# Experts' rows by indirect DMA: gathered from DRAM, and seven of sixteen pairs' outputs scattered to a DRAM table and added at the end

## The chip, the cores and the metric

The kernel runs on one core of one Trainium2 chip. The metric is the device time of one execution in microseconds, as the median of three runs. The profile is of one further execution; its times are counted from the first instruction.

## The reference, cut to what matters

One transformer block over 512 tokens of width 1024. A hybrid mixer (a short convolution, a sparse attention, a gated delta rule) adds to x; then a mixture of experts adds to it. The change is about the experts:

```python
h = rms_norm(x, norm_ffn)                       # x: 512 x 1024, after the mixer
grp = argmax(h @ w_rg + b_rg)                   # one of 4 groups of 8 experts
top_p, top_i = top_k(softmax(le[grp]), 2)       # two experts of that group
gate = top_p / sum(top_p) * p_grp
for each expert e and each token t that chose it:
    y[t] += gate[t, e] * (silu(h[t] @ w_eg[e]) * (h[t] @ w_eu[e])) @ w_ed[e]
out = x + y                                     # 32 experts, 1024 x 512, 1024 x 512, 512 x 1024 each, float32
```

## The kernel before

Tokens lie on the 128 partitions in four tiles (t = 0 to 3). The mixer's stages take the first 630 us; TensorE is kept busy in them by products of the input with w_in, w_gate and w_branch, with the attention and the delta rule in between. The delta rule (from L371) goes over four chunks c; its scaling factors are small operations on POOL (L333 to L386). The order of each engine's instructions is made when the kernel is built: the framework places an instruction when its inputs, by a simulated timeline, are there, and goes by program order among those that are ready. So what the program writes later can be placed earlier on an engine that is idle.

Routing (L922 to L1019): for each tile t the residual x1 is completed, split into a high and a low float32r part (h2h, h2l), the logits are made, two experts are chosen (oh), and `pos` gets each token's place within its expert (L939). An expert has room for CAP = 64 tokens; a loop at the end (L1252) handles those beyond, and does nothing for these inputs unless an expert has more.

Experts: for a group q of four experts, `choose` (L931) makes a 0/1 selection matrix pm (128 tokens x 256 places) for each t, and `gather_t` (L1044) multiplies h2h and h2l with it, so that TensorE itself collects the rows, already transposed, into PSUM (pxg); `chosen` copies them to SBUF with the gain (xT). `slots_info` (L1180) multiplies the same matrices with the tokens' numbers, scales and gates (pi). The first group's rows are collected before the loop (L1063).

`ffn_up` (L1079) makes gate and up products of one expert side by side into pgu, then silu on ScalarE and the product with the gate on DVE; its `turn` transposes the result. `ffn_down` (L1120) multiplies with w_ed, the two halves of 512 columns side by side in pd; y is split over ScalarE and DVE (`y_parts`, L1113), and `selection` makes a 0/1 matrix of places x tokens. When two experts have their y, `combine` (L1137) lists eight steps (four tiles t, two halves of the columns); each `combine_step` is two products (pc, L1146) and an addition to x1 on DVE (L1148). The steps are woven one by one into the products of the next experts (L1087, L1127).

Weights come in tiles of 1 MB on SyncE's queue (`wchunk`, L1032), six for an expert, into 15 places that the earlier stages have left free; a place is loaded again when TensorE has read it. The last expert's w_ed comes in three pieces, and each piece is combined and stored by itself (L1237 to L1247).

## Time and profile before

| what | value |
|---|---|
| median of 3 runs | 1253.99 us (1253.55 to 1256.53) |
| profiled execution, its own time | 1255.8 us |
| its span, first to last instruction | 1253.7 us |
| granted TensorE clock, mean | 0.994 |
| TensorE busy | 1210.6 us (97%) |
| DVE, ACT, POOL busy | 652.0, 340.6, 62.2 us |
| DMA | 258.17 MB, mean 206 GB/s |

Busy time is time in which the profile shows an instruction of the engine. Matmuls are pipelined, so two of them overlap in the records. A wait is put down to what ended it. PE is TensorE, DVE VectorE, ACT ScalarE, POOL GpSimd, SP SyncE; PEld are weight loads, and a q behind a name is the engine's queue.

### The profile page before, as it was taken

Reading aid. Unit: us, or ns where it says so; the run is one execution under the profiler, and the core shown is the slowest. Engines: PE = TensorE matmul, PEld = TensorE weight load, DVE = VectorE, ACT = ScalarE, POOL = GpSimd, SP = SyncE. Lnnn points to the kernel's source line nnn. Section 1 sums busy time; section 2 is a strip of 40 time slices with the busy share of each in tenths; the row PEclk is TensorE's granted clock in tenths of the full one; section 3 lists DMA queues with packets and bytes.
Section 4 is the critical chain, followed back from the end, with each engine's and each line's share of the span. In section 5 each row is a group of like instructions: output and inputs, shape, how many; then the busy total and the mean of one; then the engine's idle time right before and its main releaser. Section 6 shows DMA issues by size and latency. Waiting matters only on the chain.

```text
span 1253.7 us, 16998 instructions
## 1 busy us (share of the span) xinstructions
PE 1210.6 (97%) x6727; PEld 778.2 (62%) x6728; DVE 652.0 (52%) x1536; ACT 340.6 (27%) x654; POOL 62.2 (5%) x99
## 2 busy tenths in 40 slices
PE   6999999999999999999999999999999998999987
PEld 5887889877888877668996353535353443534333
DVE  5874865865448655643566352534334343333433
ACT  5443433433335446742341101010100101010111
POOL 1001303100100000000040000000000000000000
PEclk9999999999999999999999999999999999999998
DMA  5322332122233221017706999899879889798851
GB/s 211 104 84 85 101 115 93 65 84 68 71 92 97 72 68 35 1 65 286 301 11 234 421 371 395 324 417 379 345 263 354 357 325 382 283 354 324 332 199 69
DMA packets 46435, 258.17 MB, mean 206 GB/s; under 512 B 5008, under 2 KB 8976, under 8 KB 22032
## 3 DMA queue, kind: packets, MB, share of 16 engines
q1 hardware_dynamic: 44928, 254.95, 54.2%
q10 hardware_dynamic: 1424, 2.09, 0.5%
q8 instruction: 54, 0.88, 0.3%
q14 instruction: 29, 0.24, 0.1%
HBM read 254.93 MB, written 2.10 MB: 205 GB/s over the span
## 4 chain that ended last, share of the span: by engine, by line
PE 91%; DVE 4%; ACT 2%; issue 1%; DMA 1%; POOL 0%; SPq 0%; ACTq 0%; POOLq 0%; DVEq 0%
PE pgu L1083 14%; PE pd L1126 8%; PE pmm L183 8%; PE pmm L181 8%; PE pmm L182 8%; PE pgu L1082 7%; PE pc L1146 5%; PE po L818 3%; PE pxg L1045 2%; PE pxg L1046 2%; PE ptp L812 2%; PE pb L182 2%; PE pb L181 2%; PE pb L183 2%; PE pmn L543 1%; PE pmn L541 1%
## 5 line engine op out<-in xcount | busy, mean ns | idle before, releaser
L1082 PE MATMUL pgu<-we,xT 128*64 128x512 f32 x512 | 241.9, 605 | 0.0
L1083 PE MATMUL pgu<-we,xT 128*64 128x512 f32 x512 | 235.8, 602 | 0.0
L183 PE MATMUL pmm<-hTh,lo 128*128 128x512 f32 x432 | 172.1, 398 | 0.2 <-DVE lo L176 0.2
L181 PE MATMUL pmm<-hTh,hi 128*128 128x512 f32 x432 | 171.1, 396 | 0.0
L182 PE MATMUL pmm<-hTl,hi 128*128 128x512 f32 x432 | 170.6, 395 | 0.0
L176 DVE TENSOR_TENSOR lo<-raw,hi 128x1024 fp32r<-128x1024 f32 x82 | 100.5, 1226 | 115.3 <-ACT hi L175 114.1
L175 ACT CAST hi<-raw 128x1024 fp32r<-128x1024 f32 x82 | 86.1, 1050 | 165.3 <-PE pmm L182 96.0
L1148 DVE TENSOR_TENSOR x<-pc,x 128x512 f32<-128x512 f32 (+2 forms) x132 | 83.8, 669 | 82.4 <-PE pc L1146 81.9
L1083 PEld LDWEIGHTS pgu<-we,xT 128*64 128x64 f32 x512 | 64.9, 137 | 97.4 <-issue 95.6
L1126 PE MATMUL pd<-we,aT 128*64 128x512 f32 x496 | 121.3, 599 | 0.0
L1093 ACT ACTIVATE act<-pgu,rss 64x512 f32<-64x512 f32 x32 | 21.8, 681 | 339.8 <-PE pgu L1083 330.2
L1146 PE MATMUL pc<-y,sel 128*128 128x512 f32 (+2 forms) x264 | 86.9, 430 | 12.6 <-DVE y L1116 9.1
L1146 PEld LDWEIGHTS pc<-y,sel 128*128 128x128 f32 x264 | 42.8, 188 | 84.9 <-DVE y L1116 29.3
L183 PEld LDWEIGHTS pmm<-hTh,lo 128*128 128x128 f32 x432 | 81.5, 189 | 18.0 <-DVE lo L176 1.7
L181 PEld LDWEIGHTS pmm<-hTh,hi 128*128 128x128 f32 x432 | 81.7, 189 | 16.7 <-DVE fa L691 0.8
L182 PEld LDWEIGHTS pmm<-hTl,hi 128*128 128x128 f32 x432 | 81.5, 189 | 16.6
L1082 PEld LDWEIGHTS pgu<-we,xT 128*64 128x64 f32 x512 | 63.2, 137 | 42.6 <-issue 40.0
L1116 DVE TENSOR_TENSOR y<-pd,y 64x512 fp32r<-64x512 f32 (+2 forms) x68 | 44.7, 657 | 71.4 <-ACT y L1115 70.8
L1115 ACT CAST y<-pd 64x512 fp32r<-64x512 f32 (+2 forms) x68 | 37.7, 555 | 153.8 <-PE pd L1126 110.3
L1126 PEld LDWEIGHTS pd<-we,aT 128*64 128x64 f32 x496 | 34.5, 136 | 57.1 <-issue 52.8
L1094 DVE SCALAR_TENSOR_TENSOR act<-pgu,gsl,act 64x512 f32<-64x512 f32 x32 | 24.2, 757 | 79.1 <-ACT act L1093 78.7
L1045 PE MATMUL pxg<-pm,h2h 128*128 128x256 f32 x224 | 55.5, 287 | 0.0
(763 smaller groups left out, 1919.7 us busy)
## 6 DMA issues: line engine op xcount, KB each, us to landing
we<-in_w_eg_dram SPq DMA_DIRECT2D x64, 1024.0 KB, 8.6
we<-in_w_eu_dram SPq DMA_DIRECT2D x64, 1024.0 KB, 7.2
we<-in_w_ed_dram SPq DMA_DIRECT2D x62, 1024.0 KB, 8.2
raw<-in_w_in_dram SPq DMA_DIRECT2D x30, 512.0 KB, 3.7
raw<-in_w_gate_dram SPq DMA_DIRECT2D x24, 512.0 KB, 3.6
raw<-in_w_branch_dram SPq DMA_DIRECT2D x12, 512.0 KB, 3.6
raw<-in_w_nat_dram SPq DMA_DIRECT2D x8, 512.0 KB, 4.2
w<-in_cmp_w_dram SPq DMA_DIRECT2D x8, 512.0 KB, 3.8
```

The costliest lines, as they stand in the source:

```text
L175: A.copy(out=hi, in_=raw)
L176: V.tensor_tensor(out=lo, in0=raw, in1=hi.bitcast(F32), op=ALU.subtract)
L181: T.matmul(ps, ahi(k), bhi(k), start=start and k == 0, stop=False)
L182: T.matmul(ps, ahi(k), blo(k), start=False, stop=False)
L183: T.matmul(ps, alo(k), bhi(k), start=False, stop=stop and k == n - 1)
L1045: T.matmul(px, h2h[t // 2][:, t % 2, k * P:(k + 1) * P], sel, start=start, stop=False)
L1082: T.matmul(pgu[0:64], xs(k), wg(k), start=k == 0, stop=k == KT - 1)
L1083: ins = T.matmul(pgu[64:128], xs(k), wu(k), start=k == 0, stop=k == KT - 1)
L1116: V.tensor_tensor(out=y[lo, cols], in0=pd[hi], in1=y[hi, cols].bitcast(F32), op=ALU.subtract)
L1126: T.matmul(pd[64 * a:64 * a + 64], aT[:, k], wd(k, a), start=k == 0, stop=k == 3)
L1146: T.matmul(pc[:, 0:n], sel[:, t * P:(t + 1) * P], y[:, cols], start=i == 0, stop=i == len(src) - 1)
L1148: V.tensor_tensor(out=xo, in0=pc[:, 0:n], in1=xo, op=ALU.add)
```

## The change

Experts are now taken in pairs e and e + 16. The residual rows x1 are stored to a DRAM table x1rows during the routing. Each token's two choices are turned into slot numbers (isl), and eight indirect DMAs scatter the token's number, scale, gate and output row into eight DRAM tables (islots), which are zeroed early and read back and added into `info`. From it come the token numbers of each pair's 128 places (tix) and the output rows (yix); empty places get an index outside the table. Pairs 0 and 1 still get their rows from TensorE by h2h, h2l and pm0; for the other 14 `next_input` gathers the rows from x1rows by one indirect DMA, transposes them in eight pieces and multiplies by the gain. It is called for pair p + 1 behind the first down product of pair p.

For pairs 0, 2, 4, ..., 12 y is copied once and scattered, for each expert by one indirect DMA, to the DRAM table yrows (a row of 512 for each token, choice and half), which is zeroed in the delta-rule stage at c == 1. At pair 14 `add_rows` reads it back in eight loads and adds it to x1. The other nine pairs are combined on TensorE as before, eight steps for a pair. Three more places for weight tiles (yhi, ylo, h2lp) are used, which h2h and h2l leave after the first selection. All the indirect DMAs, the zero fill and the read-back of yrows are issued by POOL; the stores of x1rows and the read-back of islots by ScalarE.

```diff
+    islots = [tc.dram_tile([2 * CAP * (NEXP // 2), 4], F32, name=f"islots{i}") for i in range(2 * NT)]
+    x1rows = tc.dram_tile([S, D], F32, name="x1rows")
+
+    yrows = tc.dram_tile([2 * S * 2, 512], F32, name="yrows")
...
+        if c == 1:
+            zero = lp.tile([P, 2 * D], F32, tag="ylo", name="zero")
+            G.memset(zero, 0.0)
+            G.dma_start(yrows.rearrange("(p r) n -> p (r n)", p=P).rearrange("p (b n) -> p b n", b=4),
+                        zero.unsqueeze(1).to_broadcast([P, 4, 2 * D]))
+            for tab in islots:
+                G.dma_start(tab.rearrange("(p r) d -> p (r d)", p=P), zero[:, 0:64])
...
+    G.memset(inf, 0.0)
+    G.tensor_copy(ti[:, :, 0], C("tokm"))
     for i in range(2):
-        V.tensor_copy(ti[:, :, i], C("tokm"))
+        G.tensor_copy(inf[:, :, i, 0], C("tokm"))
+        G.tensor_copy(tg[:, :, i, 0], C("tokm"))
+        G.tensor_scalar(out=inf[:, :, i, 3], in0=C("tokm"), scalar1=float(S * i), scalar2=None, op0=ALU.add)
...
+        nc.scalar.dma_start(x1rows[t * P:(t + 1) * P], x1)
...
+    for i in range(2):
+        V.tensor_tensor(out=posh, in0=oh[i], in1=pos, op=ALU.mult)
+        V.tensor_reduce(out=psl[:, :, i:i + 1], in_=posh, axis=AX.X, op=ALU.add)
...
-    V.tensor_copy(gt2[:, :, :, 0], oh[0])
-    V.tensor_tensor(out=gt2[:, :, :, 1], in0=oh[0], in1=gt2[:, :, :, 0].bitcast(F32), op=ALU.subtract)
-    V.tensor_copy(ti[:, :, 2], rs4)
-    V.tensor_tensor(out=ti[:, :, 3], in0=rs4, in1=ti[:, :, 2].bitcast(F32), op=ALU.subtract)
...
+    half, at_p, at_e, over = (slt[:, i] for i in range(4))
+    V.tensor_scalar(out=half, in0=exi, scalar1=-16.0, scalar2=None, op0=ALU.is_ge)
+    V.tensor_scalar(out=over, in0=psl, scalar1=float(CAP), scalar2=4096.0, op0=ALU.is_gt, op1=ALU.mult)
+    V.scalar_tensor_tensor(out=at_p, in0=half, scalar=float(CAP), in1=psl, op0=ALU.mult, op1=ALU.add)
+    V.scalar_tensor_tensor(out=at_p, in0=at_p, scalar=-1.0, in1=over, op0=ALU.add, op1=ALU.add)
+    V.scalar_tensor_tensor(out=at_e, in0=half, scalar=-16.0, in1=exi, op0=ALU.mult, op1=ALU.add)
+    V.tensor_scalar(out=at_e, in0=at_e, scalar1=32.0, scalar2=None, op0=ALU.add)
+    V.scalar_tensor_tensor(out=isl, in0=at_p, scalar=16.0, in1=at_e, op0=ALU.mult, op1=ALU.add)
+    for j, tab in enumerate(islots):
+        t, i = j // 2, j % 2
+        G.indirect_dma_start(out=tab, out_offset=bass.IndirectOffsetOnAxis(ap=isl[:, t, i:i + 1], axis=0), in_=inf[:, t, i],
+                             in_offset=None, bounds_check=2 * CAP * (NEXP // 2) - 1, oob_is_err=False)
...
+    slots += [(lp, "yhi"), (lp, "ylo"), (mp, "h2lp")]
...
+    def pair_input():
+        return gp.tile([P, KT, 2 * CAP], F32, tag="xT", name="xT", bufs=3)
+
+    itab = pair_input().rearrange("p k s -> p (k s)")[:, 0:512].rearrange("p (j c) -> p j c", c=64)
+    for j, tab in enumerate(islots):
+        nc.scalar.dma_start(itab[:, j], tab.rearrange("(p e) c -> p (e c)", p=P))
+    info = mp.tile([P, NEXP // 2, 4], F32, name="info")
+    V.tensor_reduce(out=info.rearrange("p e c -> p (e c)"), in_=itab.rearrange("p j c -> p c j"), axis=AX.X, op=ALU.add)
+
+    tix = mp.tile([P, NEXP // 2], I32, name="tix")
+    V.tensor_scalar(out=tix, in0=info[:, :, 0], scalar1=4096.0, scalar2=None, op0=ALU.add)
+
+    yix = mp.tile([P, 2, NEXP // 2], I32, name="yix")
+    for h in range(2):
+        for a in range(2):
+            V.tensor_scalar(out=yix[64 * a:64 * a + 64, h], in0=info[64 * h:64 * h + 64, :, 3], scalar1=2.0,
+                            scalar2=8192.0 + a, op0=ALU.mult, op1=ALU.add)
...
+    pi = ps_e.tile([P, 2, 4], F32, tag="pt", name="pi")
+    for b in range(2):
+        for t in range(NT):
+            T.matmul(pi[:, b], row4(pm0, t)[:, P * b:P * b + P].bitcast(F32), tg[:, t, b], start=t == 0, stop=t == NT - 1)
+    info0 = mp.tile([P, 2, 4], F32, name="info0")
+    V.tensor_copy(info0, pi)
+    inputs = [pair_input() for _ in range(2)]
...
+    def next_input(pair):
+        xg = ringa.tile([P, D], F32, tag="raw", name="xg", bufs=2)
+        if pair < 4:
+            G.memset(xg, 0.0)
+        G.indirect_dma_start(out=xg, out_offset=None, in_=x1rows,
+                             in_offset=bass.IndirectOffsetOnAxis(ap=tix[:, pair:pair + 1], axis=0),
+                             bounds_check=S - 1, oob_is_err=False)
+        xT = pair_input()
+        for h in range(2):
+            pt = ps_mm.tile([P, 4, P], F32, tag="mm", name="pxg")
+            for k in range(4):
+                T.transpose(pt[:, k], xg[:, 4 * h + k::KT], ident)
+            V.tensor_tensor(out=xT[:, 4 * h:4 * h + 4], in0=pt,
+                            in1=gain[:, 4 * h:4 * h + 4].unsqueeze(2).to_broadcast([P, 4, P]), op=ALU.mult)
+        inputs.append(xT)
...
+        if to is not None:
+            y = ep.tile([P, D], F32, tag="y", name="yd", bufs=2)[:, 0:512]
+            A.copy(out=y, in_=pd)
+            G.indirect_dma_start(out=yrows, out_offset=bass.IndirectOffsetOnAxis(ap=to, axis=0), in_=y, in_offset=None,
+                                 bounds_check=4 * S - 1, oob_is_err=False)
+            return
...
+    def add_rows():
+        for i in range(2):
+            for t in range(NT):
+                yr = ringa.tile([P, D], F32, tag="raw", name="yr", bufs=2)
+                G.dma_start(yr, yrows[2 * S * i + 2 * P * t:2 * S * i + 2 * P * t + 2 * P].rearrange("(p a) n -> p (a n)", a=2))
+                x1 = x1p[t // 2][:, t % 2]
+                V.tensor_tensor(out=x1, in0=yr, in1=x1, op=ALU.add)
...
-    for q in range(NEXP // 4):
-        if q:
-            pm, xT = expert_inputs()
-            with tc.issue_after(last) if q == 1 else ExitStack():
-                for t in range(NT):
-                    choose(pm, q, t)
-            for kk in range(KT // 2):
-                px = ps_mm.tile([P, 2, 256], F32, tag="mm", name="pxg")
-                for i in range(2):
-                    for t in range(NT):
-                        gather_t(px[:, i], 2 * kk + i, t, row4(pm, t), t == 0, t == NT - 1)
-                chosen(xT, px, kk)
...
+    by_rows = range(0, 14, 2)
+    for pair in range(NEXP // 2):
+        xT, up = inputs[pair], []
+        for h in range(2):
+            es = slice(h * CAP, (h + 1) * CAP)
+            e = pair + 16 * h
+            up.append(ffn_up(lambda k: xT[:, k, es], *weights_up(w_eg[e], w_eu[e]), 
+                             lambda: slot_info(info0[:, pair], es, 2 + h) if pair < 2 else slot_info(info[:, pair], es),
+                             up[0][0] if up else None))
+        for h in range(1 if pair == NEXP // 2 - 1 else 2):
+            ffn_down(up[h][1], weights_down(w_ed[pair + 16 * h]), up[h][2],
+                     None if h else up[1][0], yix[:, h, pair:pair + 1] if pair in by_rows else None)
+            if h == 0 and len(inputs) == pair + 1 < NEXP // 2:
+                next_input(pair + 1)
+            if h == 0 and pair == by_rows[-1] + 2:
+                add_rows()
+        if len(rows) == 2:
+            combine()
+            rows.clear()
```

In the loop for overfull experts x1 is loaded again from x1rows, since h2h and h2l are gone by then.

## Rows read from the trace of the kernel before

**Rows 1.** The page's head and its slices of the span: the busy tenths of each of 40 slices of 31.3 us for TensorE and the DMA engines, and the rate of the DMA engines.

```profile
span 1253.7 us, 16998 instructions
PE   6999999999999999999999999999999998999987
...
DMA  5322332122233221017706999899879889798851
GB/s 211 104 84 85 101 115 93 65 84 68 71 92 97 72 68 35 1 65 286 301 11 234 421 371 395 324 417 379 345 263 354 357 325 382 283 354 324 332 199 69
```

**Rows 2.** Stretches of the second half: us from and to, their length, busy time (and instructions) of TensorE, its weight loads, DVE, ACT and where it is listed POOL, the granted clock, the DMA engines' busy share and their rate.

```profile
640.00:660.00 20.00, 19.89 (x170) 19.46 (x169) 16.26 (x34) 12.55 (x24) 15.71 (x13) 1.00 0.16 52
660.00:680.00 20.00, 17.67 (x118) 13.92 (x119) 16.88 (x86) 1.25 (x4) 1.37 (x2) 0.91 0.41 161
...
880.00:1205.00 325.00, 308.22 (x1383) 130.44 (x1381) 125.44 (x277) 31.96 (x52) 0.00 (x0) 1.00 0.88 337
676.00:1205.00 529.00, 512.22 (x2361) 219.28 (x2359) 214.51 (x484) 55.33 (x89) 0.00 (x0) 1.00 0.89 350
```

**Rows 3.** Waits between 880 and 1200 us, first TensorE's and then those of SyncE's DMA queue: who waited for whom, us in total, times, the longest.

```profile
PE pc L1146 <- DVE y L1116: 7.0, 12, 0.7
PE pt L1100 <- DVE act L1094: 6.2, 4, 1.6
PE pc L1146 <- DVE x L1148: 2.9, 7, 0.5
...
SPq L1038 <- PE pgu L1082: 195.2, 35, 8.1
```

**Rows 4.** Stretches again, the columns as in group 2 (the last row, of 200 us, counts only the instructions of L1045, and its last two columns are the DMA engines').

```profile
690.00:700.00 10.00, 10.00 (x47) 3.46 (x44) 3.60 (x13) 1.11 (x2) 0.00 (x0) 1.00 1.01 420
...
900.00:910.00 10.00, 8.15 (x32) 2.56 (x28) 3.19 (x6) 2.32 (x4) 0.00 (x0) 1.00 1.01 425
...
680.00:880.00 200.00, 23.65 (x96) 18.14 (x96) 1.00 0.94 379
```

**Rows 5.** TensorE's instructions in order of time around the second group's selection: start, us, line, tile written and read, shape, count. The block's first and last rows.

```profile
728.10 0.39 PE L1045 MATMUL pxg<-pm,h2h 128*128 128x256 f32 x1
...
735.71 0.28 PE L1046 MATMUL pxg<-pm,h2l 128*128 128x256 f32 x1
735.83 0.50 PE L1187 MATMUL pi<-ti,pm 128*128 128x4 f32 x4
...
737.60 0.64 PE L1082 MATMUL pgu<-we,xT 128*64 128x512 f32 x1
```

**Rows 6.** The chain that ended last, where a combine step stands between products (start, us, what), and from the page the group of the products of L1082.

```profile
739.54 0.67 PE pc L1146 x2
740.21 0.57 PE pgu L1082
...
740.78 0.42 PE pgu L1082
...
L1082 PE MATMUL pgu<-we,xT 128*64 128x512 f32 x512 | 241.9, 605 | 0.0
```

**Rows 7.** Eight transposes of 128 by 128 in the routing stage, TensorE in order of time.

```profile
657.73 1.07 PE L915 MATMUL pt<-c_ident,x 128*128 128x128 f32 x8
```

**Rows 8.** Two of DVE's instructions in order of time between the routing and the first expert, and ScalarE's longest wait there (from the waits between 656 and 690).

```profile
673.37 0.22 DVE L1016 CAST gt<-oh 128x128 fp32r<-128x128 f32 x1
673.62 0.29 DVE L1017 TENSOR_TENSOR gt<-oh,gt 128x128 fp32r<-128x128 f32 x1
...
ACT L1093 <- DVE rss L1073: 17.5, 1, 17.5
```

**Rows 9.** SyncE's issues of weights: from the instructions of L1038 the issues by tensor (w_ed and w_eu; w_eg has 64 too) with their shortest, median and longest time and their first and last start; from the issues in order of time the first one and the last that come before 676 us (15 in all).

```profile
L1038 SPq DMA_DIRECT2D we<-in_w_ed_dram x65: 327/328/1193, 602.9 to 1200.4; - x65
...
L1038 SPq DMA_DIRECT2D we<-in_w_eu_dram x64: 327/328/1500, 564.0 to 1192.2; - x64
...
557.51 0.43 SPq L1038 DMA_DIRECT2D we<-in_w_eg_dram  x1
...
659.89 0.85 SPq L1038 DMA_DIRECT2D we<-in_w_eg_dram  x2
```

**Rows 10.** The end of the chain that ended last, before the stores.

```profile
1243.96 0.33 DVE y L1116
...
1244.32 1.97 DVE x L1148 x5
```

**Rows 11.** POOL in order of time: a memset of the delta-rule stage, and the first operation of that stage's chain with the idle time before it.

```profile
0.79 0.31 POOL L435 MEMSET ue<- 128x256 f32 x1
...
119.45 0.20 POOL L333 TENSOR_SCALAR nr<-nr 128x4 f32<-128x4 f32 x1 [102.39 <-DVE nr L339]
```

**Rows 12.** From the DMA issues: KB each and median us from issue to landing; then the shortest, median and longest time to landing of all weight tiles.

```profile
raw<-in_w_gate_dram SPq DMA_DIRECT2D x24, 512.0 KB, 3.6
...
xp<-in_x_dram SPq DMA_DIRECT2D x4, 512.0 KB, 6.4
...
DMA to landing us min/median/max: 4.9/8.1/17.2
```

**Rows 13.** One expert's down products, TensorE in order of time, and a stretch behind idle time of TensorE (columns as in group 2).

```profile
1198.47 3.65 PE L1126 MATMUL pd<-we,aT 128*64 128x512 f32 x16
...
1222.68:1226.20 3.52, 3.52 (x11) 1.08 (x12) 2.06 (x11) 0.00 (x0) 0.00 (x0) 0.52 0.00 0
```

More of the change, by code (lines that the diff above doesn't have):

```diff
@@ L865 @@
     h2l = [ringa.tile([P, D], F32R, tag="raw", name="h2l", bufs=2) for _ in range(2)]
-    h2l += [mp.tile([P, D], F32R, tag=f"h2l{t}", name="h2l") for t in range(2)]
+    h2lp = mp.tile([P, 2, D], F32R, tag="h2lp", name="h2lp")
+    h2l += [h2lp[:, t] for t in range(2)]
     wr = mp.tile([P, KT, 36], F32, name="wr")
@@ L1118, with ffn_down @@
     halves = [slice(512 * a, 512 * a + 512) for a in range(2)]
-    def ffn_down(aT, wd, tok, between=None):
+    def ffn_down(aT, wd, tok, between=None, to=None):
         pd = mpsum("pd")
```

107 lines of the change are left out of this document (43 added, 64 removed).

## Prediction

> **What bounds the kernel now.** I read first the page's slices for where the time lies, then the stretches of the second half, then the waits there, then single instructions in order of time. The slices show TensorE at nine tenths or more in nearly all of them and the DMA engines nearly idle in the first half but at seven to nine tenths in the second [rows 1]. The second half is the expert stage: from 676 us, when the first expert's products start, to the end of the span at 1253.7, that is 577.7 us. There TensorE is busy 512.2 of the first 529 us at full clock, while the DMA engines are busy 0.89 and move 350 GB/s [rows 2]. The waits say which of the two ends last: TensorE never waits for a weight tile (we); between 880 and 1200 it waits 16.1 us in all, for DVE (y, x, act), while SyncE, which issues the weights, waits most of the time for TensorE to free a tile [rows 3]. So TensorE sets the pace, but with little to spare: in ten-microsecond pieces where enough tiles are free the DMA engines are full and move 420 to 425 GB/s [rows 4]. A gain on TensorE ends where the weights' own floor begins. That floor is the second sum below.
>
> **TensorE's sum.** Removed first: the selection of the rows. For each group of four experts TensorE makes 64 products (pxg) and 16 small ones (pi) in one block, 728.10 to 737.60 [rows 5]: 9.5 us. Seven groups go (the first stays): 7 x 9.5 = 66.5 us.
>
> Removed second: the combine of seven pairs. A pair has 8 steps of two products (pc). One step takes 0.67 us, and the product behind it takes 0.57 in place of 0.42 [rows 6], so 0.82 us; 7 x 8 x 0.82 = 46 us. Of the waits for y and x, 9.9 us in 320 of the stage's last 374 us, about 12 in all, 7/16 go with them: 5 us.
>
> Added: 14 pairs' rows are turned by 8 transposes. Eight of L915 took 1.07 us [rows 7], so 15 us. The new ones read every eighth element, which no row shows; a bound above is twice that, 30, and below, the 15. I take 15, since loading the operand is a separate, overlapped record there. The first two pairs' info products are now plain float32, which stand as two records each in the trace (512 of L1082 for 256 in the program) [rows 6], where the old ones took 1.8 us [rows 5]: +2 us. Before the first product DVE is busy 16.9 of 20 us [rows 2]; it gets some 11 small operations (psl, the slot numbers) like the two for gt that it loses, 0.22 and 0.29 us [rows 8]. At most 11 x 0.25 - 0.5 = 2.2 us, at least 0 if they run behind xT; I take 2.
>
> TensorE's path: 577.7 - 66.5 - 46 - 5 + 15 + 2 + 2 = 479 us, so the end at 676 + 479 = 1155.
>
> **The weights' sum.** 193 issues carry 192 MiB, 201.3 MB; 15 of them are out before 676 [rows 9], so 185.6 MB remain. The change adds traffic: 512 tokens times 2 give 1024 rows of 4 KB, 14/16 of them gathered (3.7 MB), 7/16 scattered (1.8), 4.2 MB read back, 0.3 for slot tables: 10 MB (empty slots carry indices outside the table and move nothing). 195.6 MB at 420 GB/s are 466 us. From 676 that is 1142, and behind the last weights come their products, y, the additions and the store: in the trace the last y starts at 1243.96 and the span ends at 1253.7 [rows 10], 10 us. So 1152. The three added weight tiles (yhi, ylo, h2lp) let three more issues out as soon as the first gather is done, near 675; they fill the gap in which the DMA engines now wait for the first freed tile, and are why I let the stream run from 676 without a hole.
>
> **The sum.** The floors lie 3 us apart, and neither can be reached when both bind: each wait of TensorE frees a tile later, and each late tile makes it wait. The stretch in which TensorE never waited for anything, 680 to 880, moved 379 GB/s [rows 4]; at that rate 195.6 MB take 516 us, ending at 1202. Between 1152 and 1202 I take 400 GB/s, 489 us: 676 + 489 + 10 = 1175 as a span. The profiled execution took 1255.8 around a span of 1253.7, the median of the runs is 1253.99: within 0.3 us of the span. So **1175 us**; the likeliest case's own range is 1150 to 1202.
>
> A rule speaks against it: the Trainium skill, "DMA: Bandwidth & Descriptors", section Bandwidth, says that transfers from HBM to SBUF are bound by the memory side at about 358 GB/s for a core. By that rate, as an estimate, 195.6 MB would take 546 us and the end would be 1232. The trace does not agree over ten microseconds [rows 4].
>
> **What I cost at nothing, and its cover.** The zero fill and its nine GpSimd issues: POOL sits idle 102 us before the first of the delta-rule's operations at 119.45, and it runs that stage's other memset already at 0.79 us [rows 11]. If the issues sit in front of the chain at 119 instead, nine of them at SyncE's 0.33 to 1.5 us [rows 9] and a memset eight times L435's 0.31 us cost 5.5 to 16 us, once. The stores of x1rows go out on ScalarE's queue while the DMA engines are busy 0.16 [rows 2]. The eight slot scatters and their read-back are needed first by pair 2's gather, more than 30 us later; but the read-back sits on ScalarE's queue, and behind it waits the first silu, now idle 17.5 us for its scale [rows 8]. Below nothing: none; above: eight issues at 1.5 us and a landing of 6.4 [rows 12], 18.4 us, less the 17.5, so 1 us. I take 0. The scatters of y replace two halves of y on ScalarE and DVE by one copy; POOL does nothing else in the stage. DVE loses 56 additions and gains 28 gain products and 8 additions twice as long; it is busy 214.5 of 529 us [rows 2] and stays off the path.
>
> **The rivals.**
> *The gather is waited for.* The transposes for pair p+1 stand on TensorE behind the first down product of pair p, and the kernel gives TensorE one order. If the gather is issued only then, it is covered by the second expert's down products, 3.65 us [rows 13]. Beyond that TensorE stands still, and behind such idle the trace shows the clock at half: 3.52 us at 0.52 granted (near the 1.2 of its two levels of 1.2 and 2.4 GHz) after the gaps near 1222, 1.75 us lost [rows 13]. For a gather no row exists; the nearest are loads of 512 KB, 3.6 to 6.4 us from issue to landing, and the 1 MB weights, 8.1 median and 17.2 at most [rows 12]. At 6.4: 14 x (6.4 - 3.65 + 1.75) = 63 us, 1155 + 63 = 1218. At 17.2: 14 x 15.3 = 214, 1369, **slower than before**. It decides from a landing near 9 us: 14 x (9 - 3.65 + 1.75) = 99. For it: the weights' queue will be full and the gather shares the engines. Against it: xg has two buffers, so the gather can go out a pair ahead, and POOL has only the scatter ahead of it.
> *The clock alone.* If TensorE now waits for weights in small pieces, each half-clock piece of 1.75 us counts; 45 of them, three for each pair, eat 79 us: 1254, no change. For it: the waits will be there by the second sum. Against it: from 880 to 1200 TensorE idles up to 2 us in ten and the clock stays at 1.00 [rows 4].
> *The memory gives no more than it gives now.* If the 350 GB/s of the stage [rows 2] were a ceiling for a long stretch, 195.6 MB take 559 us: 1245. The full ten-microsecond pieces speak against it. (The rule of the Trainium skill quoted above, "DMA: Bandwidth & Descriptors", section Bandwidth, would be such a ceiling.)
> *Better than both sums.* Fewer waits than I kept, weights at 425: 1140 to 1150.
>
> **How the numbers follow.** The forecast 0.60 (1150 to 1202); gather waited for in part 0.12 (1202 to 1250); gather waited for beyond the 9 us 0.10 (over 1258); the clock 0.05 (near 1254; a fifth of it still faster); the ceiling 0.05 (1245); better 0.08. The range 1142 to 1238 holds the first, most of the second and of the last: about 0.79. A measurement of this kernel tells 0.3% from no change, so 1250.2 to 1257.8 is "same": faster 0.60 + 0.12 + 0.05 + 0.08 + 0.01 = 0.86, same 0.04, slower 0.10.
>
> **What would show it.** TensorE's products pxg of L1045 and L1046 gone but for 64, pc from 264 to about 152, and transposes near 0.13 us each; DMA share near 0.95 with about 400 GB/s from 680 on; SyncE waiting less for TensorE, and TensorE for we. The expert stage should last near 500 us and the stages before 676 be unmoved within 5 us. I am wrong if transposes wait for xg by microseconds, if the clock is below 0.97 in the stage, if the rate stays near 350 with the queue full, or if POOL's issues hold up the delta rule near 120 us.

## The result, and the profile after

The changed kernel takes 1219.8 us (median) where the kernel before, run beside it, takes 1254.7: a ratio of 0.972, 95% interval 0.970 to 0.974. It is faster, by 35 us; forecast were 79 us (1175). The time lies in the wide range (1142 to 1238), outside the likeliest case's own (1150 to 1202). The median is over four executions, one of which fell into the slow state (1817 us at a granted clock of 0.56); the three fast ones lie between 1218.4 and 1220.9. The profiled execution took 1220.9 us around a span of 1219.1, so the account below has 1219 - 1175 = 44 us to explain.

The page after, as [rows 1] (40 slices, here of 30.5 us):

```profile
PE   0899999999999999999999889997997989797985
...
PEclk9899999999999999999999889999998989898997
DMA  8133233212213221200781679999999999999953
GB/s 328 56 101 90 70 104 124 93 62 87 70 53 114 87 71 51 55 16 13 257 328 74 242 274 418 420 418 419 419 418 420 420 420 419 419 419 418 412 215 122
```

Three things differ. The first slice is empty on TensorE (six tenths before) and eight tenths full on the DMA engines (five before). From slice 25 on the DMA engines are full for some 400 us at 418 to 420 GB/s, where they had a ragged seven to nine tenths. And in the last two slices they are at five and three tenths while TensorE too is below nine: a tail in which neither is full.

Stretches of the span after, as [rows 2] (us from, to and length; busy time and instructions of TensorE, its weight loads, DVE, ACT, POOL; granted clock; DMA share; GB/s):

```profile
680.00:720.00 40.00, 30.40 (x180) 23.13 (x181) 28.64 (x151) 4.18 (x10) 16.18 (x25) 0.79 0.68 247
720.00:1120.00 400.00, 360.27 (x1574) 132.21 (x1571) 113.29 (x256) 40.15 (x66) 26.45 (x26) 0.95 1.01 419
...
1160.00:1170.00 10.00, 8.65 (x37) 2.98 (x37) 4.70 (x9) 1.61 (x3) 0.58 (x1) 1.00 0.94 340
1170.00:1175.00 5.00, 4.03 (x21) 1.43 (x19) 1.18 (x2) 0.23 (x1) 0.00 (x0) 1.00 0.49 185
1175.00:1180.00 5.00, 4.96 (x26) 1.78 (x26) 4.16 (x12) 0.00 (x0) 0.69 (x2) 1.00 0.02 6
1180.00:1230.00 50.00, 21.74 (x104) 12.10 (x98) 22.95 (x38) 3.42 (x9) 2.53 (x5) 0.80 0.32 106
```

TensorE's waits between 760 and 1120 us, as [rows 3] (who waited for whom, us in total, times, the longest):

```profile
PE pgu L1162 <- DMA we<-in_w_eg_dram: 29.1, 5, 8.3
PE pgu L1163 <- DMA we<-in_w_eu_dram: 4.4, 5, 2.2
```

And those of SyncE's queue from 700 us to the end:

```profile
SPq L1085 <- DMA we<-in_w_ed_dram: 118.5, 52, 3.6
...
SPq L1085 <- PE pgu L1163: 13.6, 11, 4.4
```

Before, TensorE never waited for a weight tile and SyncE waited 195 us for TensorE [rows 3]. Now TensorE waits for weights ten times, in five pairs of waits, 33.5 us in all, and SyncE waits above all for its own earlier transfers (118.5 us for those of w_ed alone): what sets the stage's pace has changed, as the second sum had it.

The stage's edges are where the 44 us lie. TensorE's first expert product starts at 710.42, 34.4 us later than the forecast's 676 (23.5 of them are there when the first selection product starts, at 686.45 instead of 662.90). From there to 1173, where the DMA engines fall idle (half of the stretch 1170 to 1175), are 463 us; forecast were 489 at 400 GB/s, so 26 less (195.6 MB at 419 GB/s are 467 us, so the rate makes 22 of them; when the stretch starts, 18 weight tiles have been issued and not 15). From 1173 to 1219 are 46; forecast were 10, so 36 more. 34.4 - 26 + 36 = 44.4.

**The start.** POOL after, in order of time (start, us, line, operation, what is written and read, count, in brackets the idle time before it and what ended it):

```profile
1.55 1.81 POOL L389 MEMSET zero<- 128x2048 f32 x1
...
3.92 0.87 POOL L390 DMA_DIRECT2D yrows<-zero  x1
4.71 3.79 POOL L393 DMA_DIRECT2D islots<-zero  x7
25.88 0.54 POOL L393 DMA_DIRECT2D islots<-zero  x1 [17.37 <-DMA yrows<-zero]
26.55 2.31 POOL L207 TENSOR_TENSOR sc<-sc,mhalf 128x1 f32<-128x1 f32 x3
```

The zero fill is written at c == 1 of the delta rule; as its inputs are there at once, the order puts it at the start. Eight DMAs go out; the ninth stands 17.4 us, until the first, the 4 MB fill, has landed. Behind it in POOL's order stands the pow of L207, the scale of x's first rows. TensorE's first transpose, after and before:

```profile
28.51 2.82 PE L223 MATMUL pt<-c_ident,xp 128*128 128x128 f32 x12 [28.51 <-DVE xp L212]
8.49 1.97 PE L217 MATMUL pt<-c_ident,xp 128*128 128x128 f32 x8 [8.49 <-DVE xp L206]
```

**Between routing and experts.** DVE in order of time after the selection, in the kernel after:

```profile
704.64 0.17 DVE L1125 COPY info<-pi 128x8 f32<-128x8 f32 x1 [3.65 <-PE pi L1123]
...
705.84 0.98 DVE L1156 TENSOR_SCALAR tok<-info 64x1 f32<-64x1 f32 x6
706.85 0.88 DVE L1189 TENSOR_SCALAR sel<-c_moe,tok 128x512 fp32r<-128x512 f32 x2
707.65 1.12 DVE L1129 TENSOR_SCALAR xT<-pgu,prm 128x128 f32<-128x128 f32 x4
```

And TensorE there:

```profile
702.55 2.05 PE L1123 MATMUL pi<-tg,pm 128*128 128x4 f32 x16
710.42 1.08 PE L1162 MATMUL pgu<-we,xT 128*64 128x512 f32 x1 [5.82 <-issue]
```

The selection products take until 702.5, 16 us for the 12.7 of before, some of them at half clock (0.58 granted from 695 to 702.5). TensorE ends the small info products at 704.6 and stands 5.8 us: DVE copies the info and makes slot operations and two selections (sel) before the gain products that xT needs.

**The end.** POOL's loads of the table in order of time:

```profile
1122.14 0.59 POOL L1227 DMA_DIRECT2D yr<-yrows  x1 [18.50 <-PE pxg L1144]
1160.03 0.58 POOL L1227 DMA_DIRECT2D yr<-yrows  x1 [37.29 <-PE pxg L1144]
1178.71 0.54 POOL L1227 DMA_DIRECT2D yr<-yrows  x1 [18.11 <-DVE x L1229]
...
1185.22 0.54 POOL L1227 DMA_DIRECT2D yr<-yrows  x1 [4.83 <-DVE x L1229]
...
1193.30 0.54 POOL L1227 DMA_DIRECT2D yr<-yrows  x1 [2.01 <-DVE x L1229]
```

They take the two buffers of tag raw in turn with xg. The second load waits 37.3 us until pair 15's rows are transposed, the others for the addition two ahead of them: a chain of loads and additions to 1198. The last transpose of aT (L1180) is at 1183.7 and the end 35.4 us later; before the two lay 20.6 us apart.

Of the forecast's other steps, these came out. TensorE's groups of the stage after (count, busy us, mean ns, idle time before and what ended it):

```profile
L1240 PE MATMUL pc<-y,sel 128*128 128x512 f32 (+2 forms) x152 | 51.6, 450 | 10.5 <-DVE x L1242 6.4 <-DVE y L1196 3.7
L1144 PE MATMUL pxg<-c_ident,xg 128*128 128x128 f32 x112 | 18.9, 300 | 1.7 <-DVE x L1242 1.7
```

POOL's groups:

```profile
L1137 POOL DMA_INDIRECT xg<-x1rows,tix x14 | 14.3, 1023 | 88.5 <-PE pxg L1144 69.8 <-DVE xT L1145 12.0 <-DVE yix L1110 4.6
L1215 POOL DMA_INDIRECT yrows<-yd,yix x14 | 14.2, 1013 | 274.6 <-ACT yd L1214 266.8 <-DMA yrows<-yd,yix 6.2 <-issue 1.7
```

152 products pc; 112 transposes of gathered rows in 18.9 us for the 15 forecast (1.35 for a set of eight, 1.07 in [rows 7]); a gather's issue takes 1.02 us of POOL, a scatter's 1.01. A gather lands 9.0 us after its issue (median), and no TensorE wait for xg stands in the profile.

### The profile page after: what moved, and what is told of

It is laid out like the page before. It is cut to its first block, busy times and chain, and to the rows that moved or that the text cites. A ratio compares the mean times of both kernels' runs of the same rounds, so it can differ in the third digit from the quotient of the medians.

```text
span 1219.1 us, 15948 instructions
## 1 busy us (share of the span) xinstructions
PE 1115.0 (91%) x6167; PEld 717.7 (59%) x6168; DVE 590.3 (48%) x1406; ACT 332.3 (27%) x640; POOL 117.1 (10%) x172
## 5 line engine op out<-in xcount | busy, mean ns | idle before, releaser
L1162 PE MATMUL pgu<-we,xT 128*64 128x512 f32 x512 | 245.1, 627 | 37.8 <-DMA we<-in_w_eg_dram 29.1
L1163 PE MATMUL pgu<-we,xT 128*64 128x512 f32 x512 | 240.6, 619 | 4.5 <-DMA we<-in_w_eu_dram 4.4
L1162 PEld LDWEIGHTS pgu<-we,xT 128*64 128x64 f32 x512 | 69.8, 143 | 130.2 <-issue 105.9
L1163 PEld LDWEIGHTS pgu<-we,xT 128*64 128x64 f32 x512 | 69.5, 142 | 63.2 <-issue 48.8
L1173 ACT ACTIVATE act<-pgu,rss 64x512 f32<-64x512 f32 x32 | 21.8, 681 | 274.0 <-PE pgu L1163 181.4
L189 PEld LDWEIGHTS pmm<-hTh,lo 128*128 128x128 f32 x432 | 81.6, 189 | 17.9 <-DVE lo L182 1.8
L188 PEld LDWEIGHTS pmm<-hTl,hi 128*128 128x128 f32 x432 | 81.6, 189 | 16.5
L1181 DVE COPY aT<-pt 128x256 f32<-128x256 f32 x32 | 13.5, 423 | 127.8 <-PE pt L1180 127.8
L1240 PE MATMUL pc<-y,sel 128*128 128x512 f32 (+2 forms) x152 | 51.6, 450 | 10.5 <-DVE x L1242 6.4
L1242 DVE TENSOR_TENSOR x<-pc,x 128x512 f32<-128x512 f32 (+2 forms) x76 | 46.0, 656 | 22.4 <-PE pc L1240 21.8
L1240 PEld LDWEIGHTS pc<-y,sel 128*128 128x128 f32 x152 | 26.3, 198 | 44.5 <-DVE y L1196 14.4
L1195 ACT CAST y<-pd 64x512 fp32r<-64x512 f32 (+2 forms) x40 | 21.2, 537 | 104.5 <-PE pd L1206 53.6
L1215 POOL DMA_INDIRECT yrows<-yd,yix x14 | 14.2, 1013 | 274.6 <-ACT yd L1214 266.8
## 6 DMA issues: line engine op xcount, KB each, us to landing
we<-in_w_eg_dram SPq DMA_DIRECT2D x64, 1024.0 KB, 20.6
we<-in_w_ed_dram SPq DMA_DIRECT2D x62, 1024.0 KB, 20.9
```

The source lines that it names most:

```text
L188: T.matmul(ps, ahi(k), blo(k), start=False, stop=False)
L189: T.matmul(ps, alo(k), bhi(k), start=False, stop=stop and k == n - 1)
L1162: T.matmul(pgu[0:64], xs(k), wg(k), start=k == 0, stop=k == KT - 1)
L1163: ins = T.matmul(pgu[64:128], xs(k), wu(k), start=k == 0, stop=k == KT - 1)
L1173: A.activation(at, qk(pgu[0:64]), AF.Silu, scale=rss[0:64])
L1240: T.matmul(pc[:, 0:n], sel[:, t * P:(t + 1) * P], y[:, cols], start=i == 0, stop=i == len(src) - 1)
```

## The experiments

Each is the changed kernel with the edit shown, cut to what matters, timed against the kernel before on the same chip, whose median was 1253.6 to 1255.6 in all of them. Times are medians; the interval is that of the ratio to the kernel before.

### The start

```diff
-            G.dma_start(yrows..., zero...)
             for tab in islots:
                 G.dma_start(tab..., zero[:, 0:64])
+            G.dma_start(yrows..., zero...)
```

> The eight small fills of islots are issued ahead of the 4 MB fill of yrows; nothing else changes. Theory: in the changed kernel POOL's ninth DMA issue stands 17.4 us until the first one (the 4 MB fill) has landed, and the scale of the first rows of x (L207, pow) is behind it in POOL's order, so the first TensorE transpose starts at 28.5 instead of 8.5 us. With the order turned round the ninth issue waits for a small fill: the first transpose at 10 to 14 us, the time 1201 to 1205 (15 to 19 us less). Rival (the 4 MB fill takes the DMA engines from the loads of x and of the first weights, and that is what delays the start): the first transpose stays beyond 20 us and the time within 5 us of 1220.

1202.9 us (0.960, 0.958 to 0.962), 17 less than the changed kernel. POOL's order:

```profile
3.92 4.43 POOL L391 DMA_DIRECT2D islots<-zero  x8
10.07 0.74 POOL L392 DMA_DIRECT2D yrows<-zero  x1 [1.71 <-DMA islots<-zero]
10.94 1.62 POOL L207 TENSOR_TENSOR sc<-sc,mhalf 128x1 f32<-128x1 f32 x3
```

The ninth issue still waits for the first, but the first is now small: 1.7 us. The time is as expected; the first transpose is not. It comes at 17.34, because the pow still stands behind nine issues until 10.9 and DVE's order then has casts of constants ahead of x. The theory holds for the 17.4 us, and a second, smaller loss is left.

```diff
-            G.tensor_tensor(out=xt, in0=xt, in1=nmix, op=ALU.mult)        # L209
+            first4 = G.tensor_tensor(out=xt, in0=xt, in1=nmix, op=ALU.mult)
...
+            with tc.issue_after(first4.ins):
                 G.memset(zero, 0.0)
...
```

> The memset and the nine fills are kept behind L209's product on POOL, so behind three of the four scales of x; nothing else changes. Theory (POOL's order makes the loss, not the fill's traffic): first transpose at 8 to 10 us as before the change, and the start's whole 20 us come back: 1199 to 1203. If the fill's wait then only moves onto the scale of the fourth row block (its pow stands behind the fill), TensorE has the first three blocks' work meanwhile, and some 5 us may stay: 1205. Rival (traffic): the fill now meets the first weights, TensorE waits for hi/lo in the first 60 us and the time stays above 1210.

1196.9 us (0.955, 0.953 to 0.956): 23 less. The first transpose is at 8.72. POOL's order here:

```profile
17.86 0.89 POOL L391 DMA_DIRECT2D yrows<-zero  x1
18.75 3.74 POOL L394 DMA_DIRECT2D islots<-zero  x7
34.02 0.54 POOL L394 DMA_DIRECT2D islots<-zero  x1 [11.53 <-DMA yrows<-zero]
```

The ninth issue waits 11.5 us again for the 4 MB, and now nobody stands behind it. The fill itself, issued at 17.9, costs nothing that can be seen. The loss was POOL's order, and 23 us of the 44 come back with it.

### The end

```diff
-    by_rows = range(0, 14, 2)
+    by_rows = range(0, 12, 2)
```

> Six pairs are scattered instead of seven (pair 12 is combined by TensorE again), and so the read-back of the table (add_rows) runs at pair 12 instead of pair 14. Theory (the 37 us from the last weights to the end are made by add_rows: its loads take the two raw buffers in turn with xg, wait for pair 15's transposes, and its eight load-add pairs run one behind the other after the weights have ended): the eight additions end before pair 15, the stretch from the last transpose of aT (L1180) to the end shrinks from 35 to 20 to 25 us, the time is 1205 to 1211, although TensorE gets 8 more steps of 0.82 us (6.6 us). Rival (the tail is long because the last weights land late and TensorE's clock is at half there): the tail stays at 33 us or more and the time is 1219 to 1226.

1233.9 us (0.983, 0.981 to 0.985): 14 more, where 9 to 15 less were expected. The stretch behind the last transpose is short (1211.5 to 1233.3, 21.8 us), but TensorE's waits from 1100 to 1170 are these:

```profile
PE pc L1240 <- DVE x L1242: 14.5, 3, 8.9
PE pxg L1144 <- DMA xg<-x1rows,tix: 7.0, 1, 7.0
```

The chain of loads and additions has moved into the stage. DVE waits in its order for each load (first addition 1096.6, last 1151.9), the steps' additions to x stand behind them and TensorE behind those; and a gather, which needs a raw buffer too, lands late. The prediction of this run was wrong because it moved the chain and left it a chain.

```diff
-            if h == 0 and pair == by_rows[-1] + 2:
-                add_rows()
```

> The eight loads of the table and their additions are left out (so the rows of the seven scattered pairs are missing from the output); fill and scatters stay. After c_six the theory reads: the read-back is one chain of eight load-add pairs through two buffers, and whatever DVE and TensorE have behind it waits, wherever it stands. Without it the stretch from the last transpose of aT to the end falls from 35 to 20 to 23 us (it was 20.6 before the change) and the time to 1202 to 1208. Rival (the late landing of the last weights and TensorE's half clock make the tail): the stretch stays above 30 us, the time is 1215 to 1220.

The eight loads and additions are left out. 1205.8 us (0.961, 0.959 to 0.963): 14 less; the stretch behind the last transpose (1183.34) is 20.4 us. The rival falls.

```diff
     def add_rows():
         for i in range(2):
-            for t in range(NT):
-                yr = ringa.tile([P, D], F32, tag="raw", name="yr", bufs=2)
-                G.dma_start(yr, yrows[...])
-                V.tensor_tensor(out=x1, in0=yr, in1=x1, op=ALU.add)
+            for t2 in range(2):
+                yr = wchunk([P, 2, D], yrows[...])         # SyncE, a weight tile
+                todo.extend(...)                           # one addition at each combine step
...
+        if pair == NEXP // 2 - 1:
+            add_rows()
...
-            if h == 0 and pair == by_rows[-1] + 2:
-                add_rows()
```

> The table is read back by SyncE in four loads of 1 MB into four weight tiles, issued ahead of pair 15's weights, and its eight additions go to DVE one at a time between TensorE's steps, behind pair 14's combine. Theory: no chain is left; the stretch from the last transpose of aT to the end is 20 to 24 instead of 35 us; but 3 of the 4.2 MB now stand in front of the last weights, 7 us at 420 GB/s: 1206 to 1214 in all. Rival (the additions themselves, 9.8 us of DVE, make the tail wherever they stand): 1217 or more.

1207.9 us (0.964, 0.962 to 0.965), 12 less, with the whole computation; 20.9 us behind the last transpose (1185.38). So 12 of the read-back's 14 us come back when it leaves its two buffers. The edit also moves the loads to SyncE's queue and behind pair 14, and the additions between the combine steps, so what each of these gives is not separated.

```diff
# b_late and k_slots together
```

> Both edits together: the fill kept behind the first scales of x (as in b_late) and the table read back through four weight tiles (as in k_slots). If the start and the tail are separate losses they add: 23 us of b_late and what k_slots gains alone, so 1183 to 1192. If the start's gain is partly the tail's already (DMA engines that run earlier), less: 1192 to 1197.

1188.2 us (0.947, 0.945 to 0.949). 23 + 12 = 35 would be 1185; 32 came: start and end are separate losses and nearly add.

### Who sets the pace of the stage

```diff
         if len(rows) == 2:
-            combine()
+            if pair > 13:
+                combine()
             rows.clear()
```

> The combine steps of the seven odd pairs up to 13 are left out: 56 steps of 0.82 us, 46 us of TensorE's time in the stage (their rows are missing from the output). Theory (from 720 us on the DMA engines set the pace, at 418 to 420 GB/s; TensorE has slack): the time is 1213 to 1221, the DMA share from 720 to 1120 stays 1.01 and only TensorE's waits for weights grow. Rival (TensorE still sets part of the pace, as the first sum had it): 25 to 46 us less, 1174 to 1195.

1219.9 us: no change, though 112 products pc are gone. A stretch of its span:

```profile
720.00:1120.00 400.00, 348.95 (x1522) 123.79 (x1520) 87.72 (x216) 40.70 (x66) 26.16 (x26) 0.93 1.01 419
```

And two of TensorE's groups in it:

```profile
L1163 PE MATMUL pgu<-we,xT 128*64 128x512 f32 x512 | 243.4, 625 | 10.8 <-DMA we<-in_w_eu_dram 10.7
...
L1240 PE MATMUL pc<-y,sel 128*128 128x512 f32 (+2 forms) x40 | 15.0, 492 | 9.4 <-DVE x L1242 6.9 <-DVE y L1196 2.3
```

The rate is the same, the last transpose of aT is at 1183.5 (1183.7), and TensorE's time goes into more waits and a clock of 0.93 for 0.95. TensorE does not set the pace. (Of the 46 us of the expectation the group shows 36.6 us of busy time gone, 51.6 to 15.0.)

```diff
-            G.dma_start(yrows..., zero...)
...
-    by_rows = range(0, 14, 2)
+    by_rows = ()
...
-            if h == 0 and pair == by_rows[-1] + 2:
-                add_rows()
```

> The gather alone: rows come by indirect DMA as in the changed kernel, but no pair is scattered; all pairs are combined by TensorE as before the change, and the fill of the 4 MB table and its read-back are gone (the eight small slot tables stay). By the prediction's TensorE sum the stage is 577.7 - 66.5 + 15 + 2 + 2 = 530 us from the first expert product, which comes 20 to 25 us later than before the change (676), as a_swap and the changed kernel show it for the start with the small fills (9) and for the 11 to 13 us between selection products and experts: 676 + 22 + 530 = 1228, range 1218 to 1236. The DMA engines then have 10 - 6 = 4 MB more than before the change and are no longer full throughout. Rival (TensorE's sum is too high, and the weights set the pace here too): 1195 to 1210.

1226.3 us (0.975, 0.972 to 0.979). The first expert product is at 694.19 and the span ends at 1225.3: 531 us for the sum's 530. TensorE has no wait for weights in the stage. A stretch of it:

```profile
800.00:1120.00 320.00, 289.35 (x1224) 107.79 (x1222) 132.19 (x276) 35.43 (x58) 10.34 (x10) 0.99 0.98 396
```

The total of the TensorE sum holds where TensorE is the bound, but that it holds to a microsecond is in part luck: from the stage before (676 to 1253.7) to this one TensorE's busy time fell by 66 us (549.3 to 483.3), where the sum took off 50 for products, and its idle time grew by 19 (28.4 to 47.9; the waits for y are 19.0 instead of 9.1 us, those for act 16.5 instead of 7.8), where it had 2; and the kernel's four executions spread from 1219.8 to 1228.4. The run also tells what the scatter is worth: 6 us as it was built (1219.8, with the wait at the start and the chain at the end), which the intervals hardly tell from nothing, and 38 us with both mended (l_two), some 8.5 of which are the start's (first transpose at 17.1 here, 8.5 in l_two).

```diff
-    slots += [(lp, "yhi"), (lp, "ylo"), (mp, "h2lp")]
```

> The changed kernel without the three added weight tiles (yhi, ylo, h2lp), so 15 instead of 18. The prediction let the stream start without a hole because of them. Theory (the DMA engines set the pace): three issues of 1 MB go out later at the start of the stage, 3 MB at 420 GB/s are 7.5 us less head start: 1222 to 1229, with a lower DMA share in 680 to 720. Rival (the tiles that the first products free come early enough): 1218 to 1221.

1217.9 us (0.970, 0.968 to 0.973): no loss. The stream does start thinner (0.51 of the DMA engines and 196 GB/s from 680 to 720, for 0.68 and 247), but the last transpose is at 1181.4 and not later. TensorE's first product also came 5 us earlier (704.96), since the edit changed DVE's order too, so the two are mixed and the run doesn't tell what the three tiles are worth; the 7.5 us of head start expected of them are not there.

### The start of the stage

```diff
+    inputs = [...]                       # the 16 gain products, the last one is `last`
     pi = ...
-    V.tensor_copy(info0, pi)
-    inputs = [...]
+    with tc.issue_after(last.ins):
+        V.tensor_copy(info0, pi)
```

> On DVE the 16 gain products that make the first two pairs' xT come ahead of the copy of the info product and of the slot operations (copies of rss and gsl, tok, sel); nothing else changes. Theory: in the changed kernel TensorE has ended the gather at 704.6 and stands 5.8 us until xT is there at 710.4, since DVE first does 3 us of slot operations; with the order turned round the first expert product starts 3 to 5 us earlier after the first row-selection product, and as the weights' stream starts its tiles with it, the time falls by 3 to 5 us: 1215 to 1217. Rival (the weights' stream has its own start, by the tiles that the gather frees, and TensorE's start doesn't set the end): the first expert product is earlier but the time stays within 2 us of 1220.

1219.8 us: no change. The first expert product is at 703.85, 6.6 us earlier, and then TensorE waits:

```profile
PE pt L1181 <- DVE act L1175: 12.2, 1, 12.2
```

DVE's order in it, where that comes from:

```profile
723.58 1.03 DVE L1102 TENSOR_REDUCE info<-xT 128x64 f32<-128x512 f32 x1 [17.35 <-DMA xT<-islots]
```

Since less stands ahead of it, the reduction of the slot tables comes earlier in DVE's order, waits 17.4 us for the read-back, and act stands behind it. The loss had moved.

```diff
-        nc.scalar.dma_start(itab[:, j], ...)
+        G.dma_start(itab[:, j], ...)
...
+        if pair == 0:
+            tables()                     # the reduction, tix and yix, behind the second act
```

> h_first with its second wait taken away: the gain products come first on DVE, the read-back of the slot tables goes from ScalarE's queue to POOL's, and DVE's reduction of it stands behind the second expert's act. In h_first TensorE started 6.6 us earlier (703.85 for 710.42) and then stood 12.2 us for act, which stood behind the reduction, which waited 17.4 us for the read-back. Theory (the weights' stream can be filled earlier only if TensorE goes on freeing tiles): first expert product near 704, no wait for act over 3 us before 760, and as the DMA engines have 4 to 6 us more of full work before 760, the time falls to 1213 to 1217. Rival (the stream's start is set by something else, as h_first's unchanged time may mean): 1218 to 1222.

On top of h_first. 1211.0 us (0.965, 0.962 to 0.967), 9 less, more than the 3 to 7 expected: TensorE starts at 703.6 and has no wait for act before 760. But its last transpose is no earlier (1183.4); what is shorter is the stretch behind it (25.8 for 35.4 us), in which the table's second load now goes out at 1150.9 instead of 1160.0. So the gain shows in the read-back, which began earlier; whether that is all of it, the next runs ask.

### All together

```diff
# b_late, k_slots and m_first2 together
```

> All three edits: the fill behind the first scales (b_late), the table read back through four weight tiles (k_slots), and the start of the expert stage as in m_first2. l_two gave 1188.2; if the start of the stage counts it is 1180 to 1186, and if not 1186 to 1190.

1186.0 us (0.945, 0.943 to 0.947), 2 less than l_two, which the intervals don't tell apart. It would fit that what m_first2 gave alone was the chain's, which k_slots had already taken; but the last transposes of aT, in l_two and in l_best, say more:

```profile
1164.91 0.46 PE L1181 MATMUL pt<-c_ident,act 64*128 64x64 f32 x4
...
1155.97 0.46 PE L1184 MATMUL pt<-c_ident,act 64*128 64x64 f32 x4
```

In l_best the last one comes 9 us earlier (the first expert product 5 us, 682.13 for 687.37), and the stretch behind it is 28.2 us instead of 20.6. So the stage does end earlier, and the stretch behind it takes most of that back. How much of the 9 us is the earlier start's is open: in SyncE's queue the table's four loads stand ahead of the last five pieces of w_ed in l_two and behind all but one of them in l_best.

```diff
# l_best with
-        if pair == NEXP // 2 - 1:
-            add_rows()
```

> l_best without the four loads of the table and the eight additions (the seven scattered pairs' rows are then missing from the output). In l_best the 9 us that the start of the stage gave alone (m_first2) gave 2 on top of the other two edits. Theory: l_best's end is made by the read-back again: the table's loads wait in SyncE's queue for pair 12's last scatter (the rate falls to 260 to 284 GB/s near 1137), and the additions stand in DVE's order between the last transposes and y (TensorE waits 2.7 and 2.9 us for y, the last transpose of aT to the end takes 28 instead of 20.6 us). Then without them 15 to 22 us less: 10 from the traffic, 5 to 10 from the order: 1164 to 1171. Rival (the weights' own stream ends no earlier, the gain of the stage's start is lost before): 1172 to 1178, the traffic's 10 us alone.

l_best without loads and additions: 1180.0 us (0.940, 0.938 to 0.942). The theory said 1164 to 1171, the rival 1172 to 1178; neither holds. The read-back costs l_best 6 us, all of them behind the last transpose (1158.36 here, and 20.7 us from it to the end). Where the rest stays is seen in n_floor's stretches:

```profile
1130.00:1140.00 10.00, 6.74 (x20) 1.85 (x22) 2.97 (x6) 0.58 (x1) 0.00 (x0) 0.83 0.82 309
1140.00:1150.00 10.00, 10.00 (x39) 3.25 (x35) 2.74 (x4) 0.68 (x1) 0.00 (x0) 1.00 0.12 41
1150.00:1160.00 10.00, 10.00 (x49) 4.01 (x50) 6.42 (x16) 0.68 (x1) 0.00 (x0) 1.00 0.00 0
1160.00:1170.00 10.00, 8.62 (x70) 5.89 (x66) 7.13 (x20) 2.84 (x8) 0.00 (x0) 1.00 0.18 66
```

And TensorE's last wait for weights:

```profile
1139.65 0.64 PE L1167 MATMUL pgu<-we,xT 128*64 128x512 f32 x1 [1.40 <-DMA we<-in_w_eu_dram]
```

The DMA engines fall idle near 1141, and TensorE is busy almost without a gap for another 30 us: when the last of the last pair's up tiles is there, at 1139.65, only half of one expert's up products are done, and the rest of the two experts, the combine of the pair before, the last w_ed and the store are then 39 us. Loads that go out behind those tiles, as the table's do, are hidden under it: no 10 us of traffic can come back. No run shortens this work itself.

```diff
# l_best with
+    by_rows = range(0, 12, 2)
+        if pair == NEXP // 2 - 2:
+            add_rows()
```

> l_best with six scattered pairs and the table read back one pair earlier, ahead of pair 14's weights, when the last scatter (pair 10) has long landed; the additions then stand between the steps of pairs 14 and 15. TensorE combines one pair more (6.6 us), which by f_no_combine costs nothing while the DMA engines are full. Theory of n_floor: no dip of the rate and no addition behind the last transpose: 1177 to 1182. Rival (the combine or the additions hold TensorE up as in c_six, or the end is the traffic's alone): 1184 to 1192.

1184.8 us (0.944, 0.942 to 0.946): between the two expectations and not to be told from l_best. The order behind the last transpose is clean (20.4 us from 1163.19), but the table's 4 MB now stand ahead of the last up tiles (TensorE's last wait ends at 1147.7 for n_floor's 1139.7), and the one gain pays for the other.

```diff
# l_best with
-                V.tensor_tensor(out=x1, in0=src, in1=x1, op=ALU.add)
+                G.tensor_tensor(out=x1, in0=src, in1=x1, op=ALU.add)
```

> l_best with the eight additions on POOL instead of DVE, nothing else moved. POOL took 2.34 us for a product of this size (L209), 19 us for eight, after the first table has landed. If DVE's order in the tail is the loss, y is no longer held up and the time is 1178 to 1184; if the slower additions or the dip of the rate near 1137 are it, 1185 to 1194.

1191.2 us (0.948, 0.945 to 0.951): 5 more than l_best, with intervals that overlap. It is the second of the two cases. The trace points to the slower additions: the last transpose is where l_best has it (1156.24), and the stretch behind it is 35.4 us instead of 28.2, with POOL adding (2.37 us each) until 1169. The dip lies ahead of that, so what it costs is not seen here.

l_best and n_six leave nothing out and are 70 us faster than the kernel before, twice the change's own gain.

## Why the prediction was right and wrong

**The bound, right.** TensorE's sum (479 us) and the weights' sum (466) were to lie close together, the change to run into the weights' floor. It did: f_no_combine takes 112 products off TensorE and nothing off the time; e_gather_only, in which TensorE is the bound, keeps to its sum in total (531 for 530), with parts that offset each other. The clock rival is what the trace shows (0.95 granted from 720 to 1120, below the 0.97 that the prediction named as a sign against it; a product behind a wait for weights takes 1.11 us instead of 0.6). In that stretch it costs nothing, as TensorE has the time: in f_no_combine it is 0.93 at the same total. What it costs behind the last weights, no run separates. The gather is not waited for: issued a pair ahead, as argued, its 9.0 us to landing are covered.

**The rate, mis-sized by 22 of the 26 us in the kernel's favour.** 400 GB/s was chosen between the 420 of full pieces and the 379 of a stretch [rows 4]. With the queue always full the rate is 418 to 420 for 400 us; TensorE's lumps of waiting do not lower it. The row with enough free tiles was the one to take. The memory ceiling rival falls with it. The prediction took that rule without its condition: the Trainium skill, "DMA: Bandwidth & Descriptors", section Bandwidth, gives about 358 GB/s to each core when both cores of a memory domain stream, and has 425 GB/s measured for 16 MB with the other core idle. The trace agrees with the second figure: the one core that runs here moves 419 GB/s over 400 us. No run here shows the first.

**The tail, mis-sized by 36 us.** "Behind the last weights come their products, y, the additions and the store: 10 us" was read from the last y to the end of a kernel in which TensorE came last and the weights had long landed (the last was issued at 1200.4 [rows 9], 53 us before the end). This step failed: the 10 us are not the stretch from the last landing to the end. In the changed kernel the last tiles still have about a pair's work behind them: 36 to 38 us from the DMA engines' fall to the end even without the read-back (d_noadd: near 1168 to 1203.7; n_floor: 1141 to 1179.1). The other 10 or so are add_rows, of which the prediction counted the traffic and held that DVE "stays off the path": its eight loads through two shared buffers, and the additions in DVE's order (d_noadd -14, k_slots -12).

**The zero fill, costed at nothing.** The prediction saw POOL idle until 119 us and named the fill's issues ahead of the delta rule's chain as the risk (5.5 to 16 us). The order put them at the very start instead, ahead of x's first scale, where TensorE has nothing else to do; and they cost 20 us by a wait it had not thought of, the ninth issue's for the first's landing. The cover named was idle time; whose work stands behind the issues in POOL's order was not asked. So this term, put at nothing, failed as well; a_swap and b_late show what it was (17 and 23 us back).

**The start of the stage, +2 us forecast, 11 measured** (710.4 - 686.4 = 24.0 from the first selection product to the first expert product, 12.7 before): 3.4 us for the selection products at half clock, 2.0 for the info products behind them and 5.8 for DVE's order. It was counted in TensorE's sum only. What it is worth is open: in h_first and m_first2 TensorE's earlier start did not bring the last transpose forward (1185.3 and 1183.4 for 1183.7), in l_best it came 9 us earlier than in l_two, with another order in SyncE's queue, and at most 2 us of that reached the time.

The account of the profiled execution is closed by edges (34.4 - 26 + 36); by runs, 32 of the 44 us come back with two edits (l_two). By n_floor, which leaves the read-back out, 5 us over the forecast remain, although the weights' stretch there is shorter than forecast: that gain goes into the last pair's work behind the weights, 38 us for 10. That this work is the cause of the tail is read from the traces; no run removes it.

## What to carry over

When a change moves the bound from an engine to the DMA engines, read the tail anew: it runs from the last landing, not from the last result, and holds all the work that those bytes feed. A transfer that costs nothing in bytes can cost what stands behind its issue in that engine's order, so for each added DMA look up the next instruction on its engine, and where the planner may put it. A read-back through two shared buffers was a chain in both places tried here; give it buffers that are free. Whether it then stands ahead of the last weights or behind them made no difference that could be told (n_six, l_best).

## What the runs showed of the hardware

- A DMA issue on POOL waits when eight are out: the ninth went out only when the first had landed, 17.4 us (4 MB first), 1.7 us (32 KB first) and 11.5 us (4 MB, issued at 17.9). SyncE's queue shows the same count: each of its 130 issues between 760 and 1100 us finds seven earlier transfers that have not landed. In the trace POOL's DMAs report their landing on eight semaphores in turn, and so do SyncE's; whether the limit is the chip's or the framework's choice of eight, no run tells.
- Indirect DMAs of 128 rows: 1.0 us of POOL for the issue; to landing 9.0 us for a gather of 4 KB rows, 7.8 for a scatter of 2 KB rows, with the DMA engines full. A weight tile's landing rose from 8.2 to 20.9 us (median of w_ed), in which 419 GB/s bring 8.8 MB, some eight tiles.
- One core's DMA engines held 418 to 420 GB/s for over 400 us.
- Additions of 128 by 1024 stand at 1.23 us on DVE; on POOL they took 2.37 (n_pool).
